# The forgetting attention's causal mask: a sum on DVE and GpSimd at the diagonal blocks in place of a TensorE product

## Chip, cores and metric

One core of a Trainium2 chip runs the whole program. The metric is the device time of one execution in microseconds (us). The engines are named as the profile names them: PE (TensorE products), PEld (its weight loads), DVE (VectorE), ACT (ScalarE), POOL (GpSimd), SP (the queue that issues the loads).

## What is computed

Two transformer blocks follow each other. The first has two layers; in each, half of the mixed width is a gated linear attention ("gla") and the other half a forgetting attention ("fox") with 8 heads of 64 over 528 positions (16 meta positions and 512 of the sequence). Only the fox part is touched:

```python
def forgetting_attention(q, k, v, log_f):
    c = jnp.cumsum(log_f.astype(jnp.float32), axis=1)
    ...
    def block(inp):
        q_b, c_b, start = inp
        logits = (jnp.einsum('bqhd,bkhd->bhqk', q_b, kf)
                  + c_b[..., None] - c_k[:, :, None, :])
        q_pos = start + jnp.arange(Q_BLOCK)
        logits = jnp.where(key_pos[None, :] <= q_pos[:, None], logits, -jnp.inf)
        return jnp.einsum('bhqk,bkhd->bqhd', jax.nn.softmax(logits, axis=-1), vf)
```

A query's own gate `c_b` is the same for all its keys and falls out of the softmax, so the kernel adds the keys' gates `-c_k` and the causal mask alone.

## The kernel before

The program is a list of projection jobs. A job multiplies eight 128-row slices of a weight by the activations: `steps` (L321) issues, for each slice, three products over two halves of 264 positions, since every fp32 factor is split into a high and a low part. Loading and splitting the weights of later jobs (L272 on ACT, L273 on DVE) runs ahead of them. Between the slices `pump` takes functions from a queue and so strews the attention's small work over the projections. The final order on each engine is then made by a scheduler that works with its own model of durations; each engine runs its list in that order, and waits are put in where data or buffers demand them. Tiles named `g` come from a common pool of 64 SBUF buffers, score tiles (`foxS`) from a pool of two PSUM buffers.

The forgetting attention works on pairs of heads `p` (four per layer). Per pair, `fox_gates` multiplies a selector by the gates' sum (L550) and has ACT copy the result to SBUF (L552): `st["cb"][b]`, 128 equal rows with minus the gate of each key, for head `b` of the pair. `fox_pair` then queues ten units per pair: `fox_unit(b, j)` for two heads and five query blocks, j = 0 (the 16 meta queries) and j = 1 to 4 (128 queries each, N = 144, 272, 400 and 528 keys). That is 80 units in both layers, 64 of them with j of 1 or more. A unit has three stages. Its stages are queued so that the scores of one unit stand ahead of the transposes of the one before:

- `scores`: two products (L512, L513) add up q times the keys' high and low parts in PSUM; for j = 4 this is done in two score tiles (272 and 256 keys). A third product, of a bf16 identity and `maskb` (L572), adds -1e30 above the diagonal to the last 128 columns. DVE then adds the gates, writes the negative logits to `P` and reduces their minimum in one instruction (L573, shown as CUSTOM_DVE_ANT_0, with a short instruction behind it that reads the accumulator out). With two score tiles the second starts from the first's minimum. ACT takes the exponential and its sum (L577).
- `trans`: PE transposes P (L602 for the sequence keys, L610 for the first 128 keys; L582 for j = 0), ACT and DVE split the result into high and low parts (L607, L611, L179).
- `values`: for j = 2 and 4, PE multiplies by the values (L622), ACT and DVE put the halves together (L624, L626).

On POOL stand small jobs of the same stage: zeros (L495, L596, L538), the reciprocal roots of the norms (L187) and a subtraction with a repeated operand (L435).

The code of the functions concerned:

Of the kernel before, what the change touches and what calls it, by code (L numbers as in the profile page):

```python
# [12 lines left out]
ALU = mybir.AluOpType  # L13
AX = mybir.AxisListType

META = 16
# [20 lines left out]
class Net:  # L37
# [503 lines left out]

    def fox_gates(self, st, p):
        nc = self.nc
        st["cb"] = []
        for b in range(2):
            cb = self.G()
            for a, n in ((0, HALF), (HALF, L - HALF)):
                ps = self.PS("foxC_")
                self.pin(
                    nc.tensor.matmul(ps[:, :n], lhsT=self.sel[:, 2 * p + b, :], rhs=self.c3[:, a:a + n],  # L550
                                     start=True, stop=True))
                nc.scalar.activation(cb[:, a:a + n], ps[:, :n], AF.Copy)  # L552
            st["cb"].append(cb)

    def fox_unit(self, st, b, j, group):

        nc = self.nc
        r = 64 * b
        q0, qs = BLK[j] if j else (0, 128)
        N = q0 + qs  # L560
        parts = [(0, N)] if N <= 512 else [(0, HALF), (HALF, N - HALF)]
        u = {}

        def scores():
            P, mx = self.G(), self.S()
            col = st["sums"][:qs, 2 * j + b:2 * j + b + 1]
            for x, (a, n) in enumerate(parts):
                ps = self.PS("foxS_")
                last = a + n == N
                self.stacked_scores(ps, st["q"][b], st["kh"][b], st["kl"][b], q0, a, max(n, 256), not last)  # L570
                if last:
                    nc.tensor.matmul(ps[:, n - qs:n], lhsT=self.identb, rhs=self.maskb[:, :qs], start=False, stop=True)  # L572
                nc.vector.tensor_tensor_reduce(P[:qs, a:a + n], ps[:qs, :n], st["cb"][b][:qs, a:a + n], -1.0,  # L573
                                               3.0e38 if x == 0 else mx[:qs, 0:1], op0=ALU.add, op1=ALU.min,
                                               accum_out=mx[:qs, x:x + 1])
            m = mx[:qs, len(parts) - 1:len(parts)]
            nc.scalar.activation(P[:qs, :N], P[:qs, :N], AF.Exp, scale=-1.0, bias=m, accum_out=col)  # L577
            u["P"] = P

        def trans_meta():  # L580
            pm = self.PT("foxT_")
            nc.tensor.transpose(pm[:, :128], u["P"][:, :128], self.ident)  # L582
            PM = self.M()
            nc.vector.tensor_copy(PM, pm[:, :128])
            rc = self.S()
            nc.vector.reciprocal(rc[:META, 0:1], st["sums"][:META, b:b + 1])
            o = self.PT("foxV_")
            nc.tensor.matmul(o[:, :64], lhsT=PM, rhs=st["vm"][:, r:r + 64], start=True, stop=True)
            nc.vector.tensor_scalar(st["O"][:META, 0, r:r + 64], o[:META, :64], rc[:META, 0:1], None, op0=ALU.mult)

        def trans():
            odd = j % 2
            if odd:
                for z in "hl":
                    group[z] = [self.G(F32R)[:, :512].rearrange("p (k c) -> p k c", k=2) for _ in range((j + 1) // 2)]
                    nc.gpsimd.tensor_tensor(group[z][j // 2][:, 1, 0:128], self.ident, self.ident, op=ALU.subtract)  # L596
                group["m"] = self.G(F32R)[:, :512].rearrange("p (z c) -> p z c", z=2)
            C = slice(0, 128) if odd else slice(128, 256)
            pt = self.PT("foxT_")
            for k in range(1, j + 1):  # L600
                b0, _ = BLK[k]
                nc.tensor.transpose(pt[:, 128 * (k - 1):128 * k], u["P"][:, b0:b0 + 128], self.ident)  # L602
            pv = pt[:, :128 * j].rearrange("p (k c) -> p k c", k=j)
            for x in range(0, j, 2):
                n = min(2, j - x)
                h = group["h"][x // 2][:, :n, C]
                nc.scalar.activation(h, pv[:, x:x + n], AF.Copy)  # L607
                self.lo_sub(group["l"][x // 2][:, :n, C], pv[:, x:x + n], h)
            pm = self.PT("foxT_")
            nc.tensor.transpose(pm[:, :128], u["P"][:, :128], self.ident)  # L610
            nc.scalar.activation(group["m"][:, 0, C], pm[:, :128], AF.Copy)  # L611
            self.lo_sub(group["m"][:, 1, C], pm[:, :128], group["m"][:, 0, C])

        def values():

            vs, vms = st["vs"][b], st["vms"][b]
            o = self.PT("foxV_")
            ops = [(vms, group["m"][:, 0, :]), (vms, group["m"][:, 1, :])]
            for k in range(j):
                ops += [(vs[:, 128 * k:128 * k + 128], group[z][k // 2][:, k % 2, :]) for z in ("h", "l")]  # L620
            for x, (lt, rv) in enumerate(ops):
                nc.tensor.matmul(o[:, :256], lhsT=lt, rhs=rv, start=x == 0, stop=x == len(ops) - 1)  # L622
            tmp = self.G()
            nc.scalar.activation(tmp[:64, :256], o[64:, :256], AF.Copy)  # L624
            c0 = 128 * (j - 2)
            nc.vector.tensor_tensor(st["oT"][r:r + 64, c0:c0 + 256], o[:64, :256], tmp[:64, :256], op=ALU.add)  # L626

        if j == 0:
            return [scores, trans_meta]
        return [scores, trans] if j % 2 else [scores, trans, values]  # L630

    def fox_pair(self, st, i, p, mix, last):
# [1041 lines left out]
```

## Time and profile before

| | us |
|---|---|
| median of 3 runs | 2336.28 (2336.06 to 2337.36) |
| the profiled execution, its own time | 2338.46 |
| its span, first to last instruction | 2336.7 |
| PE busy in the span | 2311.3 |
| DVE busy | 1369.9 |
| ACT busy | 953.3 |
| POOL busy | 254.4 |

How it is read: busy time of PE runs from the first column of a product to its modelled end, and products overlap, so the time that a product takes out of PE's stream is read from the distance between the starts of its neighbours and not from its own duration. The fox units lie in two stretches, from 68 to 230 us (first layer) and from 735 to 897 us (second layer). A row of the view by windows gives the stretch, its length, the busy time and number of instructions of PE, PEld, DVE, ACT and POOL, and then the granted clock as a share of full speed, the DMA share and GB/s.

### The profile page before, as it was taken

How to read it: one execution, taken by the hardware profiler on the slowest of the kernel's cores; microseconds unless marked ns; L12 is line 12 of the kernel's file. 1: busy time of each engine (PE TensorE's matmuls, PEld its weight loads, DVE VectorE, ACT ScalarE, POOL GpSimd, SP SyncE). 2: the span in 40 equal slices, each digit the busy share in tenths (PEclk: the TensorE clock that was granted, in tenths of full speed). 3: DMA queues.
4: the chain of work that ended last, by engine and by line, in shares of the span. 5: the costliest groups of instructions: out<-in, count | busy, mean ns of one | idle time of the engine just before them, and what ended most of it. 6: DMA issues, size and time to landing. Idle time of an engine off the chain costs nothing.

```text
span 2336.7 us, 37580 instructions
## 1 busy us (share of the span) xinstructions
PE 2311.3 (99%) x15703; PEld 2126.2 (91%) x15703; DVE 1369.9 (59%) x2445; ACT 953.3 (41%) x1641; POOL 254.4 (11%) x261
## 2 busy tenths in 40 slices
PE   8999999999999999999999999999999999999998
PEld 7999999999999999999999889988999888888888
DVE  6767656465657677465565666796454454433335
ACT  6665534233347556343233534222333533322225
POOL 2111210000022112200000221100000002101012
PEclk9999999999999999999999999999999999999999
DMA  4211222222232211222223222232221222323324
GB/s 116 73 55 55 73 90 86 95 87 87 87 88 71 57 55 52 94 91 91 91 82 106 85 78 82 92 98 91 73 73 55 73 93 92 104 90 90 99 86 131
DMA packets 217072, 196.77 MB, mean 84 GB/s; under 512 B 8987, under 2 KB 214791, under 8 KB 216903
## 3 DMA queue, kind: packets, MB, share of 16 engines
q1 hardware_dynamic: 216903, 194.37, 26.7%
q8 instruction: 124, 2.03, 0.4%
q14 instruction: 45, 0.37, 0.1%
HBM read 192.26 MB, written 2.10 MB: 83 GB/s over the span
## 4 chain that ended last, share of the span: by engine, by line
PE 67%; ACT 1%; DVE 1%; issue 1%; DMA 0%; POOL 0%; POOLq 0%; ACTq 0%; SPq 0%; DVEq 0%
PE mm L321 60%; PE valuesT L1160 1%; PE scoresS L1143 1%; PE foxV L622 1%; PE attend_pT L482 1%; PE foxT L602 0%; PE foxS L512 0%; PE foxS L513 0%; DMA raw<-in_w_down_dram 0%; PE idx L512 0%; ACT wh L272 0%; PE spreadS L221 0%; PE idx L513 0%; DVE g L432 0%; PE token_sumsT L210 0%
## 5 line engine op out<-in xcount | busy, mean ns | idle before, releaser
L321 PE MATMUL mm<-g,wh 128*128 128x264 f32 (+3 forms) x9168 | 1879.0, 315 | 3.1 <-ACT wh L272 1.4
L321 PEld LDWEIGHTS mm<-g,wh 128*128 128x128 f32 x9168 | 1388.2, 189 | 103.7 <-ACT wh L272 1.7
L321 PE MATMUL mm<-g,wl 128*128 128x264 f32 (+3 forms) x4552 | 1160.0, 313 | 0.0
L321 PEld LDWEIGHTS mm<-g,wl 128*128 128x128 f32 x4552 | 750.5, 189 | 50.4
L272 ACT ACTIVATE wh<-raw 128x1024 fp32r<-128x1024 f32 (+1 forms) x369 | 384.8, 1043 | 934.2 <-PE mm L321 797.3
L273 DVE TENSOR_TENSOR wl<-raw,wh 128x1024 fp32r<-128x1024 f32 (+1 forms) x369 | 444.9, 1206 | 74.6 <-ACT wh L272 64.2
L377 DVE TENSOR_TENSOR g<-mm,g 128x528 f32<-128x528 f32 (+2 forms) x228 | 158.7, 696 | 319.7 <-PE mm L321 315.1
L204 POOL TENSOR_TENSOR g<-g,g 128x528 f32<-128x528 f32 (+3 forms) x49 | 71.6, 1472 | 900.5 <-ACT g L203 900.5
L179 DVE TENSOR_TENSOR g<-g,g 128x512 fp32r<-128x512 f32 (+3 forms) x131 | 91.7, 700 | 37.9 <-ACT g L1012 29.2
L1037 DVE TENSOR_TENSOR g<-mm,g 128x528 f32<-128x528 f32 (+1 forms) x48 | 33.6, 700 | 119.3 <-PE mm L321 119.2
L994 ACT ACTIVATE g<-g,cv 128x528 f32<-128x528 f32 (+1 forms) x88 | 72.2, 820 | 17.9 <-DVE g L377 17.7
L1423 POOL TENSOR_TENSOR g<-g,g 128x512 f32<-128x512 f32 x22 | 38.8, 1766 | 283.1 <-ACT g L1422 283.1
L997 DVE SCALAR_TENSOR_TENSOR g<-g,cv,g 128x526 f32<-128x526 f32 (+1 forms) x88 | 66.8, 760 | 3.1
L996 DVE SCALAR_TENSOR_TENSOR g<-g,cv,g 128x527 f32<-128x527 f32 (+1 forms) x88 | 66.4, 754 | 1.8 <-ACT g L994 1.8
L179 DVE TENSOR_TENSOR g<-foxT,g 128x128 fp32r<-128x128 f32 (+1 forms) x160 | 50.5, 340 | 20.3 <-ACT g L607 18.1
L1008 ACT ACTIVATE g<-g 128x528 f32<-128x528 f32 (+1 forms) x44 | 28.1, 639 | 83.8 <-DVE g L997 83.8
L187 POOL TENSOR_TENSOR sm<-sm,mhalf 128x10 f32<-128x10 f32 (+3 forms) x29 | 37.2, 1291 | 116.8 <-DVE sm L186 115.7
L1010 DVE TENSOR_TENSOR g<-g,g 128x528 f32<-128x528 f32 (+1 forms) x44 | 30.8, 701 | 32.3 <-ACT g L1008 32.3
L577 ACT ACTIVATE g<-g,sm 128x144 f32<-128x144 f32 (+2 forms) x80 | 43.1, 538 | 15.5 <-DVE sm L573 14.7
L607 ACT ACTIVATE g<-foxT 128x256 fp32r<-128x256 f32 (+1 forms) x96 | 33.2, 346 | 27.7 <-PE foxT L602 22.7
L1012 ACT ACTIVATE g<-g 128x528 fp32r<-128x528 f32 (+1 forms) x44 | 28.1, 639 | 33.1 <-DVE g L1010 33.1
L1454 DVE TENSOR_TENSOR g<-mm,g 128x512 f32<-128x512 f32 x16 | 11.1, 692 | 49.9 <-PE mm L321 49.9
(281 smaller groups left out, 1697.5 us busy)
## 6 DMA issues: line engine op xcount, KB each, us to landing
raw<-in_w_up_dram SPq DMA_DIRECT2D x50, 1024.0 KB
raw<-in_w_in_dram SPq DMA_DIRECT2D x44, 1024.0 KB
raw<-in_w_down_dram SPq DMA_DIRECT2D x28, 896.0 KB
raw<-in_w_in_dram SPq DMA_DIRECT2D x28, 512.0 KB
raw<-in_w_out_dram SPq DMA_DIRECT2D x12, 1024.0 KB
raw<-in_w_down_dram SPq DMA_DIRECT2D x12, 1024.0 KB
raw<-in_w_gate_dram SPq DMA_DIRECT2D x10, 1024.0 KB
raw<-in_w_up_dram SPq DMA_DIRECT2D x10, 512.0 KB
```

The costliest lines, as they stand in the source:

```text
L179: (eng or self.nc.vector).tensor_tensor(out, x, hi.bitcast(F32), op=ALU.subtract)
L187: self.nc.gpsimd.tensor_tensor(out, v[:rows, :n], self.mhalf[:rows, :n], op=ALU.pow)
L204: nc.gpsimd.tensor_tensor(acc[:, t0:t1], tmp[:, t0:t1], acc[:, t0:t1], op=ALU.add)
L272: keep(nc.scalar.activation(hi[:, :K], src, AF.Copy))
L273: keep(nc.vector.tensor_tensor(lo[:, :K], src, hi[:, :K].bitcast(F32), op=ALU.subtract))
L321: nc.tensor.matmul(ps[:, b, :n], lhsT=w[:, k, :], rhs=x[:, t:t + n], start=(ki == 0 and pi == 0), stop=(ki == len(order) - 1 and pi == len ...
L377: self.nc.vector.tensor_tensor(self.v(out, toks), self.psv(ps, toks), self.v(rs, toks), op=ALU.mult)
L577: nc.scalar.activation(P[:qs, :N], P[:qs, :N], AF.Exp, scale=-1.0, bias=m, accum_out=col)
L994: nc.scalar.activation(A[:, lo:], U[:, lo:], AF.Identity, bias=self.vec("cb", 44 * i + t), scale=cw(2))
L996: nc.vector.scalar_tensor_tensor(A[:, s1:], U[:, s1 - 1:L - 1], cw(1), A[:, s1:], op0=ALU.mult, op1=ALU.add)
L997: nc.vector.scalar_tensor_tensor(A[:, s0:], U[:, s0 - 2:L - 2], cw(0), A[:, s0:], op0=ALU.mult, op1=ALU.add)
L1423: nc.gpsimd.tensor_tensor(z[:, META:], z[:, META:], self.rs[:, META:], op=ALU.mult)
```

## The change

`fox_gates` makes a second tile per head, `cm`: the gates `cb` plus the causal mask `fmask` (-3e38 above the diagonal), repeated over the four 128-key blocks, by one POOL instruction of 128 x 512. In `scores` the product with `maskb` stays for j = 0 alone. For j of 1 or more the last 128 columns are cut off: DVE adds `cb` to the columns ahead of them and `cm` to these, each by an instruction of its own with its own accumulator read, the later one starting from the minimum of the earlier. Nothing else is edited.

```diff
     def fox_gates(self, st, p):
-        st["cb"] = []
+        st["cb"], st["cm"] = [], []
...
             st["cb"].append(cb)
+            cm = self.G()
+            nc.gpsimd.tensor_tensor(cm[:, META:].rearrange("p (j c) -> p j c", j=4),
+                                    cb[:, META:].rearrange("p (j c) -> p j c", j=4),
+                                    self.fmask.unsqueeze(1).to_broadcast([128, 4, 128]), op=ALU.add)
+            st["cm"].append(cm)
...
-            for x, (a, n) in enumerate(parts):
+            x = 0
+            for a, n in parts:
                 ps = self.PS("foxS_")
-                last = a + n == N
-                self.stacked_scores(ps, st["q"][b], st["kh"][b], st["kl"][b], q0, a, max(n, 256), not last)
-                if last:
+                mask = j == 0
+                self.stacked_scores(ps, st["q"][b], st["kh"][b], st["kl"][b], q0, a, max(n, 256), not mask)
+                if mask:
                     nc.tensor.matmul(ps[:, n - qs:n], lhsT=self.identb, rhs=self.maskb[:, :qs], start=False, stop=True)
-                nc.vector.tensor_tensor_reduce(P[:qs, a:a + n], ps[:qs, :n], st["cb"][b][:qs, a:a + n], -1.0,
-                                               3.0e38 if x == 0 else mx[:qs, 0:1], op0=ALU.add, op1=ALU.min,
-                                               accum_out=mx[:qs, x:x + 1])
-            m = mx[:qs, len(parts) - 1:len(parts)]
+
+                cuts = [(a, n, "cb")]
+                if j and a + n == N:
+                    cuts = [(a, n - qs, "cb"), (N - qs, qs, "cm")] if n > qs else [(a, n, "cm")]
+                for c, w, key in cuts:
+                    nc.vector.tensor_tensor_reduce(P[:qs, c:c + w], ps[:qs, c - a:c - a + w], st[key][b][:qs, c:c + w],
+                                                   -1.0, 3.0e38 if x == 0 else mx[:qs, x - 1:x], op0=ALU.add,
+                                                   op1=ALU.min, accum_out=mx[:qs, x:x + 1])
+                    x += 1
+            m = mx[:qs, x - 1:x]
```

The lists of PE, DVE, ACT and POOL change between the first fox scores of a layer and the start of its output projection; SP's does not change, and PE's is the same everywhere else. In the changed file the lines behind the edit are higher by 5 to 12: L573 becomes L584, L602 L614, L610 L622, L622 L634, L596 L608; L578 is the mask product that is left.

PE's list before, first layer, first pair of heads, from the scores of the unit b = 0, j = 3 (`foxS_1024`) on; `foxT_992` and `foxT_996` are the transposes of the unit ahead of it:

```order
L512 MATMUL foxS_1024<-g_646,g_713 128x400
L513 MATMUL foxS_1024<-g_647,g_713 128x400
L572 LDWEIGHTS identb
L572 MATMUL foxS_1024<-maskb,identb 128x128
L321 MATMUL mm_957<-g_288,wh_721 128x264 x2
L321 MATMUL mm_957<-g_289,wh_721 128x264
L602 MATMUL foxT_992<-ident,g_928 128x128
```

And after, the same place (`foxS_1028` is that unit's tile, `foxT_996` and `foxT_1000` are the transposes ahead):

```order
L512 MATMUL foxS_1028<-g_646,g_713 128x400
L513 MATMUL foxS_1028<-g_647,g_713 128x400
L321 MATMUL mm_961<-g_288,wh_721 128x264 x2
L321 MATMUL mm_961<-g_289,wh_721 128x264 x2
L321 MATMUL mm_961<-g_288,wl_722 128x264 x2
L321 MATMUL mm_961<-g_313,wh_721 128x264 x2
L614 MATMUL foxT_996<-ident,g_932 128x128
```

The weight load and the product of the mask are gone, and the earlier unit's transposes stand behind eight projection products where they stood behind three.

DVE's list before at the same place, from the last split of the earlier unit's transposes:

```order
L626 TENSOR_TENSOR g_807<-foxV_1006,g_1013 64x256
L573 ISA g_1022,sm_1023<-foxS_1024,g_815 128x400
L573 ISA sm_1023 128x1
L179 TENSOR_TENSOR g_989<-foxT_1036,g_987 128x2x128
L179 TENSOR_TENSOR g_991<-foxT_1041,g_991 128x128
L573 ISA g_1051,sm_1052<-foxS_1053,g_815 128x272
```

And after (`g_815` is `cb`, `g_822` is `cm` of head b = 0):

```order
L638 TENSOR_TENSOR g_807<-foxV_1010,g_1017 64x256
L584 ISA g_1026,sm_1027<-foxS_1028,g_815 128x272
L584 ISA sm_1027 128x1
L179 TENSOR_TENSOR g_993<-foxT_1040,g_991 128x2x128
L584 ISA g_1026,sm_1027<-foxS_1028,g_822,sm_1027 128x128
L584 ISA sm_1027 128x1
L179 TENSOR_TENSOR g_995<-foxT_1045,g_995 128x128
```

One sum over 400 columns has become one over 272 and one over 128, and a split of another unit's transposes stands between them.

POOL's list before, first pair of the first layer (L427 finishes the gates' sum, L596 are zeros for the values' stage):

```order
L427 TENSOR_TENSOR c_110<-g_526,g_596 8x528
L495 MEMSET g_653 64x528
L596 TENSOR_TENSOR g_909<-ident 128x128
L596 TENSOR_TENSOR g_911<-ident 128x128
L495 MEMSET g_939 64x528
```

And after:

```order
L427 TENSOR_TENSOR c_110<-g_526,g_596 8x528
L495 MEMSET g_653 64x528
L555 TENSOR_TENSOR g_822<-g_815,fmask 128x512
L555 TENSOR_TENSOR g_831<-g_824,fmask 128x512
L608 TENSOR_TENSOR g_913<-ident 128x128
L608 TENSOR_TENSOR g_915<-ident 128x128
L495 MEMSET g_943 64x528
```

The two sums of mask and gates stand ahead of the pair's zeros; in the rest of the list the other 14 are put in in the same way and nothing else moves.

## Rows read from the trace of the kernel before

**Rows 1.** The page, part 1: busy time of each engine over the span.

```profile
PE 2311.3 (99%) x15703; PEld 2126.2 (91%) x15703; DVE 1369.9 (59%) x2445; ACT 953.3 (41%) x1641; POOL 254.4 (11%) x261
```

**Rows 2.** The page, part 4: the chain that ended last, shares by engine.

```profile
PE 67%; ACT 1%; DVE 1%; issue 1%; DMA 0%; POOL 0%; POOLq 0%; ACTq 0%; SPq 0%; DVEq 0%
```

**Rows 3.** Fox stretches by window: length, then each engine's busy us (and instructions).

```profile
68.00:230.00 162.00, 160.99 (x1292) 152.34 (x1291) 117.74 (x340) 94.80 (x257) 24.95 (x44) 1.00 0.18 51
735.00:897.00 162.00, 161.12 (x1293) 152.60 (x1294) 118.02 (x341) 94.65 (x257) 24.76 (x43) 1.00 0.19 55
```

**Rows 4.** The mask product as a group by line: busy us, mean ns.

```profile
L572 PE MATMUL foxS<-maskb,identb 128*128 128x128 bf16 x80 | 18.4, 229 | 0.0
```

**Rows 5.** PE in order of time (start, length), with and without mask, both 272 columns.

```profile
157.87 0.29 PE L512 MATMUL foxS<-g,g 128*128 128x272 f32 x1
...
158.12 0.23 PE L572 MATMUL foxS<-maskb,identb 128*128 128x128 bf16 x1
158.16 0.73 PE L321 MATMUL mm<-g,wh 128*128 128x264 f32 x4
158.73 0.40 PE L321 MATMUL mm<-g,wl 128*128 128x264 f32 x2
158.97 0.52 PE L321 MATMUL mm<-g,wh 128*128 128x264 f32 x3
...
213.05 0.29 PE L512 MATMUL foxS<-g,g 128*128 128x272 f32 x1
...
213.30 0.65 PE L321 MATMUL mm<-g,wh 128*128 128x264 f32 x4
213.79 0.40 PE L321 MATMUL mm<-g,wl 128*128 128x264 f32 x2
214.03 0.65 PE L321 MATMUL mm<-g,wh 128*128 128x264 f32 x4
```

**Rows 6.** PE in order of time, a mask product with transposes behind it.

```profile
73.05 0.23 PE L572 MATMUL foxS<-maskb,identb 128*128 128x128 bf16 x1
73.12 0.28 PE L602 MATMUL foxT<-ident,g 128*128 128x128 f32 x1
73.24 0.27 PE L610 MATMUL foxT<-ident,g 128*128 128x128 f32 x1
73.27 0.74 PE L321 MATMUL mm<-g,wh 128*128 128x264 f32 x4
```

**Rows 7.** DVE groups of L573 by shape: busy us, mean ns, idle before.

```profile
L573 DVE CUSTOM_DVE_ANT_0 g<-foxS,g 128x272 f32<-128x272 f32 x32 | 13.8, 433 | 4.0 <-PE foxS L572 3.9
L573 DVE CUSTOM_DVE_ANT_0 g<-foxS,g 128x400 f32<-128x400 f32 x16 | 9.0, 561 | 0.0
L573 DVE DVE_READ_ACCUMULATOR2_ANT sm<- 128x1 f32 x96 | 7.9, 82 | 0.0
L573 DVE CUSTOM_DVE_ANT_0 g<-foxS,g,sm 128x256 f32<-128x256 f32 x16 | 7.7, 479 | 0.6
L573 DVE CUSTOM_DVE_ANT_0 g<-foxS,g 128x144 f32<-128x144 f32 x16 | 4.8, 302 | 1.2 <-PE foxS L572 0.7
```

**Rows 8.** All engines in order of time: an exponential and the transposes behind it.

```profile
82.60 0.62 ACT L577 ACTIVATE g<-g,sm 128x400 f32<-128x400 f32 x1
...
83.44 0.49 PE L602 MATMUL foxT<-ident,g 128*128 128x128 f32 x3
```

**Rows 9.** PE's waits, the fox stage's: total us, times, longest.

```profile
PE foxV L522 <- DVE g L377: 2.2, 3, 1.9
...
PE foxT L602 <- ACT g L611: 0.2, 1, 0.2
```

**Rows 10.** ACT and DVE in time, first pair; POOL's sum with a repeated operand as group.

```profile
68.36 0.36 ACT L552 ACTIVATE g<-foxC 128x256 f32<-128x256 f32 x1
...
70.72 0.31 DVE L573 CUSTOM_DVE_ANT_0 g<-foxS,g 128x144 f32<-128x144 f32 x1
...
L435 POOL TENSOR_TENSOR g<-g 128x512 f32<-128x512 f32 x4 | 5.8, 1438 | 5.8 <-DVE g L432 4.0 <-DVE g L437 1.7
```

## Prediction

> **What bounds the kernel now.** I read the page's first part first: PE is busy 99% of the span, DVE 59%, ACT 41%, POOL 11% [rows 1]. The chain that ended last lies on PE for 67% of the span, and no other engine has more than 1% of it [rows 2]. So time is won by taking work out of PE's stream, or lost by making PE wait. The change touches two stretches of 162 us. The view by windows shows both alike, which is as it should be, as both layers run the same code: PE busy 161 of 162 us at full clock, DVE 118, ACT 95, POOL 25 [rows 3]. What I looked for next was what one mask product takes out of that stream, and how far DVE's answer lies ahead of the transposes that need it. The waits of PE in the fox stage are short: 0.2 us in all for the transposes, 2.2 us for those of the values, and these wait for an eviction and not for the softmax [rows 9].
>
> **What is removed.** 64 of the 80 mask products (j of 1 or more), each with its weight load. The record of one says 229 ns [rows 4], but records overlap, so the price is the distance between neighbours. Two units with 272 columns give it. Without a mask (the first half of a j = 4 unit) the stretch from L512 over L513 and six projection products to the next one is 214.03 - 213.05 = 0.98 us. With the mask it is 158.97 - 157.87 = 1.10 us, six products again [rows 5]. The difference is 0.12 us. It falls in two pieces: the product behind the mask starts 0.04 us after it (158.16 - 158.12), but its group of four takes 158.73 - 158.16 = 0.57 us where the unmasked group takes 213.79 - 213.30 = 0.49 us. What the 0.08 us are made of the rows don't say, but they come with the mask and only there. Going through the 64 in order of time I find a projection product behind 52 and a transpose behind 12. For those the distance is 73.12 - 73.05 = 0.07 us, and the next transpose starts after 0.12 us [rows 6], some 0.01 more than elsewhere; I take 0.08 us. Sum: 52 x 0.12 + 12 x 0.08 = 6.2 + 1.0 = **7.2 us** off PE. The bounds: 64 x 0.04 = 2.6 us if only the first piece goes, and 64 x 0.229 = 14.7 us if the whole record counted; the latter I exclude, as rows 5 show the overlap.
>
> The Trainium skill has a figure for this (TensorE: Matmul & The Clock Gate, Back-to-back issue gap): about 81 ns for a product of 128 columns in a stream of loads and products, about 56 ns for one by itself. By these the sum would be an estimated 5.2 or 3.6 us; the trace's 0.12 us is more, and I go by the trace.
>
> **What is added on DVE.** Each of the 64 units gets one more sum and one more accumulator read. From 144 to 400 columns a sum goes from 302 to 561 ns, so 1.01 ns for a column and 156 ns for the instruction; the form that starts from an earlier minimum takes 479 ns at 256 columns, 64 ns more than that line; the read takes 82 ns [rows 7]. A cut of 128 columns with such a start is then 156 + 129 + 64 = 349 ns. For j = 2: 302 + 82 + 349 in place of 433, 0.30 us more. The other j give the same within 0.01 us. All together 64 x 0.30 = 19.2 us, 9.6 in each stretch. DVE goes from 118 to some 128 us of 162 [rows 3]: still far from full, and this is the cover. What it costs if the cover is gone is what PE's transposes wait for. The tightest place of the trace: an exponential ends at 82.60 + 0.62 = 83.22 us, and its transposes start at 83.44 [rows 8], 0.22 us later. Of the 64 units 10 have less than 0.55 us there, the others 0.65 to 27 us. If the 0.30 us passed on whole, two of them would be short by 0.08 us. In the new list of PE, however, the transposes at that kind of place have moved back (behind eight projection products instead of three), while in DVE's list a split now stands between the two sums of a unit, which adds to its delay. I take **0.5 us** for the two; if all ten paid whole it would be 3.0 us.
>
> **What is added on POOL.** 16 sums of 128 x 512 with a repeated operand, as L435, which takes 1.44 us [rows 10]: 23 us, on an engine busy 25 of 162 us. DVE waits for them in its own order, and behind it its evictions for PE. In the first pair ACT finishes the last piece of both heads' gates at 68.36 + 0.36 = 68.72 us; both sums one after the other from there end at 71.6, even without counting that the first head's are ready earlier. The first unit's masked piece is wanted at 70.72 plus the short first piece [rows 10] and needs the first sum only, done by 70.2 at the latest; the second head's first masked unit is queued two units further on. Price nought; the pair's zeros behind them on POOL are not wanted before the values. If each of the 8 pairs paid one sum, 8 x 1.44 = 11.5 us.
>
> **What is moved.** PE's list is rearranged in the two stretches, by tens of products at most, and meets the old one before the output projection. PE is idle for 1.0 and 0.9 us in them [rows 3], so a better order can give back 1.9 us at most; a worse one could double them, so also 1.9 us the other way. I take nought and keep both ends. No load is issued elsewhere, since SP's list stays.
>
> **The sum.** 7.2 - 0.5 = 6.7 us saved. It stands against the profiled execution (2338.46 us, span 2336.7), 2.2 us above the median; nothing in the two stretches hangs on that difference, so I take the saving off the median: 2336.28 - 6.7 = **2329.6 us**, 0.29% less.
>
> **The rivals.**
> - *The second piece stays.* The 0.08 us behind a mask belong to any change of the kind of product, and with the mask gone the time is lost elsewhere in the stream, so that only the first piece, 2.6 us, is won: 2333.7 us. For it: the two kinds still alternate at every transpose. Against it: the unmasked row of rows 5 has no such piece.
> - *The longer softmax holds PE now and then.* Each unit that is late costs up to 0.30 us; with 20 of 64 late, 7.2 - 6.0 = 1.2 us are left: 2335.1 us. For it: DVE's list strews other splits between a unit's sums. Against it: the slack of rows 8, small for 10 units only.
> - *DVE becomes the bound of the stage (slower).* If the two-buffer score tiles, now released later by the added sum, and the late exponentials make PE wait for the whole added 0.30 us in every unit, the loss is 19.2 us against 7.2: 2336.28 + 12.0 = 2348.3 us. It decides from 24 late units of 64 (7.2 / 0.30). For it: all scores pass through two buffers. Against it: DVE idles 44 of 162 us. The Trainium skill (VectorE: DVE Perf Modes, Rules for kernel authors) advises to lower the number of DVE instructions, as each flushes its pipe; the trace's 156 ns per instruction agrees.
> - *The change doesn't do what it says.* PE's new list has 16 mask products, those of j = 0, and no others; I give it nothing.
>
> **How the numbers follow.** A measurement of this kernel tells about 0.2%, 4.7 us, from no change. Forecast 0.63; second piece stays 0.14; late now and then 0.14; DVE the bound 0.06; and 0.03 for more than the forecast, a better order giving its 1.9 us and the mask 0.13 us (2326 us). The forecast's own range is 6.7 less the 1.9 us of the rearrangement and a little more, to 6.7 + 1.9: 2327.7 to 2331.5, all beyond 4.7 us. So faster 0.63 + 0.03 = 0.66; same 0.14 + 0.14 = 0.28; slower 0.06. To hold 8 in 10 the range needs most of the two middle rivals: 2327.5 to 2335.0 us.
>
> **What would show it.** Right: 16 records of the mask product; L512 to the product seven places on 0.98 us in j = 2 units as in unmasked ones; the fox stretches shorter by 3.3 us each and the rest unchanged; some 128 us of DVE in each; POOL's new sums near 1.4 us and done before the first sum over `cm`; PE's waits for the transposes still under 1 us in all. Wrong: waits of PE on L589's exponential or on the release of score tiles; sums over `cm` that start on POOL's release; stretches that are shorter by 1.3 us only.

## The result and the profile after

| | before | after |
|---|---|---|
| median, us | 2336.52 (6 runs, 2336.06 to 2339.97) | 2349.07 (6 runs, 2347.64 to 2351.09) |
| ratio | 1 | 1.0051 [1.0041, 1.0061] |

The changed kernel is slower by 0.51%, 12.6 us between the medians, where 6.7 us less was forecast. The page (part 1, against [rows 1]) and the windows of the fox stretches (against [rows 3]):

```profile
PE 2310.9 (98%) x15639; PEld 2127.0 (91%) x15639; DVE 1378.2 (59%) x2573; ACT 952.0 (41%) x1641; POOL 273.6 (12%) x277
```

```profile
68.00:230.00 162.00, 160.06 (x1262) 151.40 (x1262) 122.20 (x401) 93.48 (x254) 38.13 (x59) 1.00 0.20 57
735.00:897.00 162.00, 160.04 (x1259) 151.15 (x1258) 122.08 (x394) 93.06 (x252) 39.41 (x59) 1.00 0.19 55
```

In each of these windows PE idles 1 us more than before, which explains no 12 us. The loss lies just behind them. PE's waits in the fox stage (us in total, times, longest); L522 waited as long before [rows 9], the others are new:

```profile
PE foxN L695 <- DVE o L682: 4.8, 2, 2.4
PE foxV L634 <- DVE g L179: 4.5, 2, 2.3
...
PE foxV L522 <- DVE g L377: 2.2, 3, 1.7
...
PE mm L321 <- DVE g L379: 1.1, 2, 0.5
...
PE to_tokensT L708 <- DVE gvm L176: 0.7, 2, 0.4
```

Each of the new ones comes once in each layer, the two long ones (L695, L634) at the end of the last pair of heads, the two short ones further ahead. The first of the long ones in time is that of the last values. DVE, ACT and PE there (start, length, and in brackets the idle time before and who ended it):

```profile
232.44 0.42 DVE L179 TENSOR_TENSOR g<-foxT,g 128x256 fp32r<-128x256 f32 x1
233.60 1.22 DVE L273 TENSOR_TENSOR wl<-raw,wh 128x1024 fp32r<-128x1024 f32 x1 [0.74 <-ACT wh L272]
234.74 0.61 DVE L179 TENSOR_TENSOR g<-foxT,g 128x256 fp32r<-128x256 f32 x2
...
232.51 1.06 ACT L272 ACTIVATE wh<-raw 128x1024 fp32r<-128x1024 f32 x1
233.48 0.36 ACT L619 ACTIVATE g<-foxT 128x256 fp32r<-128x256 f32 x1
...
235.31 0.77 PE L634 MATMUL foxV<-g,fvms 128*128 128x256 f32 x2 [2.27 <-DVE g L179]
```

A later job's weight split (L272 on ACT, then L273 on DVE) stands between the splits of the last unit, and PE waits 2.27 us for the last of these. Before, that weight split stood nine microseconds later, at 242.84 us. The second wait is 15 us further on. DVE and POOL, then PE:

```profile
243.65 0.68 DVE L768 TENSOR_REDUCE sm<-g 128x4 f32<-128x512 f32 x1
246.13 0.69 DVE L776 TENSOR_TENSOR g<-g,sm 128x512 f32<-128x512 f32 x1 [1.81 <-POOL sm L187]
...
248.02 0.69 DVE L776 TENSOR_TENSOR g<-g,sm 128x512 f32<-128x512 f32 x1 [0.80 <-POOL sm L187]
248.63 0.70 DVE L377 TENSOR_TENSOR g<-mm,g 128x528 f32<-128x528 f32 x1
...
249.32 0.82 DVE L682 TENSOR_TENSOR o<-o,sm 128x640 f32<-128x640 f32 x1
...
243.18 2.92 POOL L187 TENSOR_TENSOR sm<-sm,mhalf 128x10 f32<-128x10 f32 x2 [0.17 <-DVE sm L186]
246.98 1.01 POOL L187 TENSOR_TENSOR sm<-sm,mhalf 128x4 f32<-128x4 f32 x1 [0.88 <-DVE sm L186]
...
250.28 0.74 PE L695 MATMUL foxN<-ident,o 128*128 128x128 f32 x5 [2.42 <-DVE o L682]
```

The scaling of the fox result (`fox_scale`, L682) stands behind two gla scalings (L776), and each of these waits for a power on POOL (1.81 and 0.80 us). PE's transposes (L695) wait 2.42 us. In the kernel before the order is the other way round, the fox scaling first:

```profile
240.89 0.83 DVE L670 TENSOR_TENSOR o<-o,sm 128x640 f32<-128x640 f32 x1
...
244.05 0.69 DVE L764 TENSOR_TENSOR g<-g,sm 128x512 f32<-128x512 f32 x1
```

A third part of the loss is the clock behind the first wait (windows; granted clock is the third number from the end):

```profile
225.00:230.00 5.00, 5.00 (x44) 4.77 (x43) 3.66 (x16) 3.46 (x11) 0.00 (x0) 1.00 0.44 153
230.00:235.00 5.00, 3.04 (x25) 2.62 (x23) 2.38 (x5) 2.26 (x5) 0.00 (x0) 0.98 0.00 0
235.00:240.00 5.00, 4.69 (x25) 4.37 (x26) 2.08 (x5) 2.14 (x4) 0.00 (x0) 0.68 0.01 2
...
245.00:250.00 5.00, 2.86 (x24) 2.64 (x22) 3.07 (x7) 1.72 (x5) 2.62 (x4) 1.00 0.00 0
```

From 235.3 us on PE works without a break and yet does 25 products up to 240 us, where it did 44 from 225 to 230: by the granted clock 3.4 us, from 234.8 us on, are at 1.2 GHz in place of 2.4. The second layer shows the same (0.66 from 907 to 912 us).

What the change was meant to do it does. The mask product is left for j = 0 alone; an unmasked j = 2 unit takes 113.40 - 112.42 = 0.98 us; the sums on DVE and POOL cost what [rows 7, 10] let one expect. PE in order of time:

```profile
112.42 0.29 PE L512 MATMUL foxS<-g,g 128*128 128x272 f32 x1
...
113.40 0.40 PE L321 MATMUL mm<-g,wh 128*128 128x264 f32 x2
```

And the groups of the mask product, DVE's sums and POOL's sums by line and shape (count, busy us, mean ns, idle before):

```profile
L578 PE MATMUL foxS<-maskb,identb 128*128 128x128 bf16 x16 | 3.7, 230 | 0.0
...
L584 DVE CUSTOM_DVE_ANT_0 g<-foxS,g,sm 128x128 f32<-128x128 f32 x80 | 27.2, 345 | 3.0 <-PE foxS L513 0.9
L584 DVE DVE_READ_ACCUMULATOR2_ANT sm<- 128x1 f32 x160 | 13.0, 82 | 0.0
L555 POOL TENSOR_TENSOR g<-g,fmask 128x512 f32<-128x512 f32 x16 | 20.3, 1288 | 153.0 <-DVE fvms L179 55.7 <-ACT g L552 50.8 <-PE foxC L550 36.3
```

### The profile page after: what moved, and what is told of

Same layout as the page of the kernel before. It is cut to its first block, busy times and chain, and to the rows that moved or that the text cites. A ratio compares the mean times of both kernels' runs of the same rounds, so it can differ in the third digit from the quotient of the medians.

```text
span 2349.0 us, 37654 instructions
## 1 busy us (share of the span) xinstructions
PE 2310.9 (98%) x15639; PEld 2127.0 (91%) x15639; DVE 1378.2 (59%) x2573; ACT 952.0 (41%) x1641; POOL 273.6 (12%) x277
## 4 chain that ended last, share of the span: by engine, by line
PE 66%; DVE 1%; ACT 1%; issue 1%; DMA 0%; POOL 0%; POOLq 0%; ACTq 0%; SPq 0%; DVEq 0%
PE mm L321 60%; PE valuesT L1172 1%; PE scoresS L1155 1%; PE foxV L634 1%; PE attend_pT L482 1%; PE foxT L614 0%; PE foxS L512 0%; DVE wl L273 0%; DMA raw<-in_w_down_dram 0%; ACT wh L272 0%; PE foxS L513 0%; PE idx L512 0%; PE to_tokensT L465 0%; PE idx L513 0%; PE spreadS L221 0%
## 5 line engine op out<-in xcount | busy, mean ns | idle before, releaser
L321 PE MATMUL mm<-g,wh 128*128 128x264 f32 (+3 forms) x9168 | 1878.1, 315 | 4.1 <-ACT wh L272 1.4
L321 PEld LDWEIGHTS mm<-g,wh 128*128 128x128 f32 x9168 | 1392.0, 189 | 103.8 <-ACT wh L272 1.7
L321 PE MATMUL mm<-g,wl 128*128 128x264 f32 (+3 forms) x4552 | 1158.3, 313 | 0.0
L321 PEld LDWEIGHTS mm<-g,wl 128*128 128x128 f32 x4552 | 751.0, 189 | 49.6
L272 ACT ACTIVATE wh<-raw 128x1024 fp32r<-128x1024 f32 (+1 forms) x369 | 384.7, 1043 | 920.4 <-PE mm L321 778.4
L273 DVE TENSOR_TENSOR wl<-raw,wh 128x1024 fp32r<-128x1024 f32 (+1 forms) x369 | 445.1, 1206 | 77.8 <-ACT wh L272 67.7
```

The lines of the kernel that those rows point to most:

```text
L272: keep(nc.scalar.activation(hi[:, :K], src, AF.Copy))
L273: keep(nc.vector.tensor_tensor(lo[:, :K], src, hi[:, :K].bitcast(F32), op=ALU.subtract))
L321: nc.tensor.matmul(ps[:, b, :n], lhsT=w[:, k, :], rhs=x[:, t:t + n], start=(ki == 0 and pi == 0), stop=(ki == len(order) - 1 and pi == len ...
```

## The experiments

**The measure.** All kernels run the same 13,720 projection products (L321) in the same order. A layer's fox part with the end of its last pair lies between the starts of the 211th and the 1401st (first layer), and of the 4901st and the 6301st (second). These two times, from each kernel's trace, the time at half clock within them, and the ratio to runs of before on the same chip:

| kernel | first, us | second, us | half clock, us | median of the runs | ratio to before |
|---|---|---|---|---|---|
| before | 227.19 | 249.56 | 3.4 + 0 | 2336.52 | 1 |
| before, again | 225.67 | 249.47 | 0 + 0 | 2337.76 | 1.0002 [0.9992, 1.0012] |
| changed | 231.99 | 256.28 | 3.4 + 3.4 | 2349.07 | 1.0051 [1.0041, 1.0061] |
| changed, again | 232.13 | 255.99 | 3.4 + 3.4 | 2348.04 | 1.0050 [1.0035, 1.0065] |
| product out | 223.69 | 247.62 | 0 + 0 | 2329.00 | 0.9966 [0.9954, 0.9978] |
| product out, again | 224.06 | 247.66 | 0 + 0 | 2329.69 | 0.9968 [0.9956, 0.9981] |
| sum cut | 226.70 | 250.81 | 0 + 0 | 2338.54 | 1.0006 [0.9997, 1.0015] |
| no POOL sums | 231.35 | 254.08 | 3.4 + 0 | 2345.26 | 1.0042 [1.0029, 1.0054] |
| both places | 226.68 | 251.20 | 0 + 0 | 2339.20 | 1.0010 [1.0001, 1.0018] |
| scale ahead | 228.67 | 253.73 | 3.4 + 3.4 | 2342.53 | 1.0025 [1.0016, 1.0034] |
| split behind | 230.92 | 255.23 | 3.4 + 3.4 | 2345.00 | 1.0035 [1.0021, 1.0048] |
| tail restored | 226.77 | 251.20 | 0 + 0 | 2335.82 | 0.9999 [0.9990, 1.0008] |
| last pair by products | 225.23 | 249.62 | 0 + 0 | 2336.65 | 0.9999 [0.9990, 1.0008] |
| whole masked gates | 225.62 | 250.25 | 0 + 0 | 2336.00 | 0.9998 [0.9989, 1.0007] |

The two profiles of the kernel before give the price of one piece at half clock: 227.19 - 225.67 = 1.5 us. Sums below are against the second one, 225.67 + 249.47 = 475.1 us.

**The product alone.** Before, with `last` in `scores` true for j = 0 only:

```diff
-                last = a + n == N
+                last = a + n == N and j == 0
```

> The kernel before without its 64 mask products of j = 1 to 4, and nothing in their place (so the causal mask inside the diagonal blocks is left out of the result). DVE, ACT and POOL have their old work, and their lists differ from the old ones by 46, 26 and no rows; the end of the last pair stands in the old order. It prices the product alone. By the prediction's term it is 7.2 us faster than before (2329.3 us, ratio 0.997). By the account of the two traces it is little: between the same two projection products the changed kernel's first stretch is 4.8 us longer with 5.45 us more idle time of PE, the second 6.9 us longer with 5.72 us more idle time and one more piece at half clock (3.4 us, so 1.7 us lost), which leaves 0.65 and 0.5 us for the products: 1.2 us faster (2335.3 us, 0.9995). If the removal alone brought the loss, it is slower by up to 12 us.

> The kernel before without its 64 mask products once more (the causal mask inside the diagonal blocks is left out of the result). Between the same projection products its two stretches were 1.8 and 1.9 us shorter than those of the kernel before, after taking 1.7 us off for the latter's piece at half clock: 3.7 us, while the medians differ by 8.0 us. If the product is worth 8 us, it is at 2328 to 2330 us again, with few pieces at half clock. If only the 3.7 us belong to it and the rest was chance, it is at 2331 to 2334 us here.

Measured twice: 8.0 and 7.7 us faster. The stretches are 3.8 and 3.4 us shorter, so 3.6 us on average. The account made from the changed kernel's trace (1.2 us in all) falls. The price of one product is what was predicted, 0.98 us for a unit that took 1.10, but part of the 7.2 us is given back in small waits of PE for the units' splits, which the trace of before has not or not so long [rows 9]. First profile of this kernel:

```profile
PE foxV L522 <- DVE g L377: 2.4, 3, 1.8
PE foxT L602 <- DVE g L179: 1.4, 5, 0.3
PE foxV L622 <- DVE g L179: 0.5, 2, 0.3
```

PE idles 6.9 us (4.1 + 2.8) in these two stretches, against 4.8 us (2.9 + 1.9) in the second profile of before: 2.1 us are given back so. A listed wait is counted from the modelled end of the product ahead; in the changed kernel the last product ahead of the wait of 2.27 us starts 2.56 us before the next, where products in a stream start 0.12 us apart, so 2.44 us are lost, 0.17 us more than listed. By this the seven new waits are an estimated 1.2 us longer than listed, and 3.6 + 2.1 + 1.2 = 6.9 us, near the 7.2.

Another 4 us of the difference of the medians these stretches don't show. 1.4 us of it is a piece at half clock near 693 us, which both profiles of before have and both of this kernel have not, behind a wait of 0.8 us that all four have. The granted clock of all runs points the same way: its mean is 0.9973 in the 37 runs of before on the two chips that this kernel ran on, and 0.9985 in this kernel's 12, so before is at half clock for some 2 x 0.0012 x 2330 = 5.6 us more. At 1.5 us for a piece of 3.4 us that is an estimated 2.5 us at most (the 1.4 among them), and so a part of the 8 us is clock and not the products' own time. Why the clock falls less often is open, and so is what is left of the 4 us.

**DVE's part alone.** Before, products kept, the sum cut:

```diff
-            for x, (a, n) in enumerate(parts):
+            x = 0
+            for a, n in parts:
...
+                cuts = [(a, n)]
+                if j and last and n > qs:
+                    cuts = [(a, n - qs), (N - qs, qs)]
+                for c, w in cuts:
```

> The kernel before with its mask products kept, and the last 128 columns of each unit's sum on DVE cut off into an instruction of their own with its accumulator read, as the change has them, over the unmasked gates. It is DVE's part alone, and the end of the last pair stands in the old order. If the added work of DVE (19 us) is what slows the changed kernel, it is 10 us or more slower than before (2347 us, ratio 1.004 or more). If the order at the end of the last pair does it, DVE's part alone costs 0 to 2 us (2336 to 2338 us, 1.000 to 1.001).

1.5 us slower by the medians, with an interval of the ratio that holds 1, and 2.4 us in the stretches (1.0 + 1.3). The added work of DVE alone is not what costs 12 us.

**POOL's part.** The changed kernel with `st["cm"].append(cb)` in place of the sum over `fmask`.

> The changed kernel without POOL's 16 sums: the cut-off sum reads the unmasked gates (so the causal mask inside the diagonal blocks is left out of the result). PE, DVE and ACT have the changed kernel's work, and the weight split and the fox scale stand at the end of the last pair where the changed kernel has them. If POOL's sums hold DVE or PE, it is back at 2330 to 2337 us (ratio to before 0.998 to 1.000). If the order does it, it stays within 2 us of the changed kernel: 2347 to 2351 us (1.0045 to 1.0062).

Still 8 us slower than before, with the same two waits. In the stretches, pieces at half clock taken off, it is 483.9 us against 485.2: POOL's 16 sums cost 1.3 us with the order that comes with them, not nothing, but not the loss. Most of it is the wait for L379 (1.1 us), which this kernel doesn't have. The median is 1.7 us under the expected range; 1.5 us of that is the piece at half clock that the second stretch doesn't have in this profile.

**The order put back at both places.** No work is changed; edges tell the scheduler what to place behind what. `fs` is the instruction of `fox_scale`, and `late` holds the last unit's splits on ACT and DVE:

```diff
     def split(self, jb, pin=False):
...
+            with ExitStack() as es:
+                for x in late[0] + late[1]:
+                    es.enter_context(self.tc.issue_after(x.ins))
+                nc.scalar.activation(hi[:, :K], src, AF.Copy)
+                nc.vector.tensor_tensor(lo[:, :K], src, hi[:, :K].bitcast(F32), op=ALU.subtract)
...
         def scale():
+            with self.tc.issue_after(self.fs.ins):
```

The first edge is on the one weight split that had come forward, the second on the gla scales. The next two kernels have the second edge alone and the first alone. In the traces of all three every engine's order is the changed kernel's up to 232 us and from 271 us on (904 and 942 us in the second layer), and POOL's is the same throughout.

> The changed kernel with two orders put back, in each layer: the weight split that went ahead of the last unit's splits stands behind them (on ACT and DVE), and the fox scale stands ahead of the gla scales that wait for POOL. Work and data are the changed kernel's. If the order at these two places does it, PE's waits there (2.27 + 2.42 us in the first layer, about as much in the second) and the piece at half clock behind the first go: 9.4 us of waits and some 3.4 us of clock, so 12 us less than the changed kernel, 2336 to 2338 us (ratio to before 1.000 to 1.001) if the product is worth about 1 us, and 2330 to 2333 us if it is worth 7. If DVE's or POOL's added work does it, it stays at 2345 us or more.

> The changed kernel with the fox scale put back ahead of the gla scales on DVE, and nothing else; the weight split stays ahead of the last unit's splits. If each of the two places costs what PE waits there, PE's wait for the fox scale (2.42 us and 2.36) goes and that for the last values (2.27 twice) stays: 5 us less than the changed kernel, 2344 us (ratio to before 1.003). If the first wait alone brings the rest with it, nothing is won: 2348 to 2350 us.

> The changed kernel with the weight split put behind the last unit's splits on ACT and DVE, and nothing else; the fox scale stays behind the gla scales. PE's wait for the last values shrinks from 2.27 us to about 0.45 (as in the run with both places), the half-clock piece behind it (3.4 us, 1.7 us lost) goes, and a wait of 1.1 us for the eviction behind the split stays, twice: 4 to 6 us less than the changed kernel, 2343 to 2345 us (ratio to before 1.0025 to 1.0035). With the run before, the two savings should add up to the 9.9 us of both places. If they don't add up, the second wait takes over what the first gives.

With both, 9.9 us of the 12.6 are back by the medians (2339.2 us, 1.2 above the expected range), with the changed kernel's DVE and POOL work untouched. So the order at the end of the last pair is the cause of the larger part. Of the single ones, the fox scale put ahead brings 6.5 us, 1.5 more than expected, the split put behind 4.1. The stretches tell more: there they bring 5.9 and 2.1 us, each with two pieces at half clock still in them, and both edges 10.4 us, with none. 3.0 of the 10.4 us are the clock, and 7.4 are left against 5.9 + 2.1: the waits' savings add up, but the clock comes back only when both waits go. One expectation on the second fell: the piece at half clock doesn't go, it moves behind the other wait. PE with the split behind:

```profile
233.57 0.50 PE L647 MATMUL foxV<-g,fvms 128*128 128x256 f32 x2 [0.45 <-DVE g L180]
236.35 0.64 PE L331 MATMUL mm<-g,wh 128*128 128x264 f32 x3 [1.11 <-DVE g L387]
247.53 0.74 PE L708 MATMUL foxN<-ident,o 128*128 128x128 f32 x5 [2.26 <-DVE o L695]
```

The wait for the values (L647 here) shrinks from 2.27 to 0.45 us, that for the eviction behind the weight split (1.11 us) takes part of its place, and the half clock starts at 249.0 us, 1.5 us behind the end of the wait for the fox scale.

**The whole end restored.** As both places, but the weight split behind the fox scale, where it stood before.

> The changed kernel with the whole end of the last pair on DVE in the order of the kernel before: the fox scale ahead of the gla scales, and the weight split behind the fox scale (on ACT behind the square), so that an eviction that PE waits for (1.1 us a layer with both places mended) doesn't stand behind the split either. If the order at the end is what is left, PE loses 1.3 to 2.0 us less in each layer than with both places mended (2339.2 us): 2335 to 2336.5 us (ratio to before 0.999 to 1.000). If what is left lies in the middle of the stage or in DVE's added work, it stays at 2338 to 2340 us.

The median is as expected, 2335.8 us, and the wait of 1.11 us is gone. But the stretches are not shorter than with both places mended (226.77 and 251.20), and the intervals of the two ratios overlap, so the 3.4 us between the medians can't be put down to that wait. What is left against product and cut together, 478.0 - (475.1 - 3.6 + 2.4) = 4.1 us, holds POOL's 1.3 us, with the wait for L389 (L379 in the changed kernel) in it, and two more waits that the kernel before has not, for the last values (L647) and at `to_tokens` (L721):

```profile
PE mm L331 <- DVE g L389: 1.1, 2, 0.5
PE foxV L647 <- DVE g L180: 0.9, 2, 0.4
PE to_tokensT L721 <- DVE gvm L177: 0.7, 2, 0.4
```

**The last pair by products.** The changed kernel, with the change left out for the last of the four pairs, so that the end falls into its old order by itself. POOL still makes all 16 sums.

> The changed kernel with the last of the four pairs of heads masked by products as before: 48 of the 64 products are gone and 48 of the sums are cut, and the order at the end of the stage is the old one. If the loss belongs to the order there, three quarters of the product's 8.0 us less the cut's 1.5 us are won, 4.9 us, and up to 2.6 us are lost at two waits in the middle of the stage: 2332 to 2335 us (ratio to before 0.998 to 0.999). If DVE's or POOL's work does it, three quarters of the loss stay: 2346 us (1.004).

The loss is gone, as it must be if the order is its cause, and the two long waits too, but the gain doesn't come: 2336.65 us, 1.7 above the expected range. The expectation was reckoned with the 8.0 us between medians. With what the stretches show, three quarters of 3.6 us are won and of 2.4 us lost, and the wait at `to_tokens` (0.7 us in all) is there: 475.1 - 2.7 + 1.8 + 0.7 = 474.9 us, and 474.9 us were measured.

**Fewer cuts.** POOL makes two masked copies of a head's gates, so that only j = 1 needs a cut: 16 new sums on DVE in place of 64, 80 instructions on POOL in place of 16. DVE's end is again in the old order.

`zm` holds 128 zero columns and the mask; `ce` gets blocks 2 and 4 masked, `co` block 3, and block 1 at its end:

```diff
-            cm = self.G()
...
+            ce, co = self.G(), self.G()
+            nc.gpsimd.tensor_tensor(co[:, 400:], cb[:, META:META + 128], self.fmask, op=ALU.add)
+            nc.gpsimd.tensor_copy(ce[:, :META], cb[:, :META])
...
+                                    self.zm.unsqueeze(1).to_broadcast([128, 2, 256]), op=ALU.add)
+            nc.gpsimd.tensor_copy(co[:, :144], cb[:, :144])
+            nc.gpsimd.tensor_tensor(co[:, 144:400], cb[:, 144:400], self.zm, op=ALU.add)
```

> All 64 products out, the mask kept, but the sums on DVE cut for j = 1 alone (16 units in place of 64): POOL makes, from the gates of a head, one tile with blocks 2 and 4 masked and one with block 3 masked, so that the sums of j = 2, 3 and 4 read one tile each, as before; POOL has 80 new instructions in place of 16, DVE 34 more than before. The end of the last pair comes out in the old order. If order is the cause of the changed kernel's loss and the added sums cost little, it keeps nearly the gain of the run without products (8.0 us), less a quarter of the cut's 1.5 us and up to 2 us for POOL: 2329.5 to 2332 us (ratio to before 0.997 to 0.998), faster than both kernels. If POOL's added work holds DVE, it is at 2336 us or more.

> The changed kernel once more, on the same chip as the run before, so that the two can be set side by side, and for a second profile of its waits and of the granted clock behind them. The two waits at the end of each layer's last pair (2.27 and 2.4 us) should be there again to within 0.1 us, as they follow from the order; the pieces at half clock may lie elsewhere. 2347 to 2351 us (ratio to before 1.004 to 1.006).

No gain: 2336.0 us, the same as before, where 2329.5 to 2332 us were expected. In the first pair POOL is now busy beside DVE's weight split, and both take longer. DVE and POOL of this kernel in order of time:

```profile
73.97 1.87 DVE L276 TENSOR_TENSOR wl<-raw,wh 128x1024 fp32r<-128x1024 f32 x1
75.76 1.64 DVE L182 TENSOR_TENSOR g<-g,g 64x528 fp32r<-64x528 f32 x2
...
73.64 2.45 POOL L618 TENSOR_TENSOR g<-ident 128x128 fp32r<-128x128 f32 x4
```

And DVE of the kernel without products, where POOL rests there:

```profile
73.62 1.23 DVE L273 TENSOR_TENSOR wl<-raw,wh 128x1024 fp32r<-128x1024 f32 x1
74.76 0.69 DVE L179 TENSOR_TENSOR g<-g,g 64x528 fp32r<-64x528 f32 x1
```

PE then waits for a split (0.95 us at 78.36 us, and 0.99 us in the second layer). In the two stretches PE idles 9.3 us, 2.4 more than without products, and they are 4.6 us longer; what makes the rest is not shown. The Trainium skill says why these two engines may hold each other (GPSIMD Engine Reference, Specifications): POOL's interface to SBUF is shared with DVE, and instructions of DVE with two SBUF inputs contend. Both of DVE's here have two, so the rows agree.

The repeat of the changed kernel has its two waits again at the same places (2.27 and 2.42 us), with the half clock at the first in both layers.

**Before, again.**

> The kernel before once more, for a second profile. The first one has pieces at half clock at 64.0, 695.5 and 1354.3 us, the run without products only at 1346.7 us, and nothing ahead of 64 us differs between the two. If the pieces belong to the kernel (its waits end at 63.8 and 693.8 us), they are there again at the same places. If they fall by chance, other ones are there, or fewer, and the time is 2335 to 2338 us all the same.

The piece at 64 us is not there again, those near 693 and 1352 us are. So a piece behind a given wait comes with some profiles and not with others, and stretches are compared without them.

## Why the prediction was wrong

- **What bounds the kernel**: right. PE is the bound, and time was lost by making it wait.
- **What is removed, 7.2 us**: the 0.12 us of a unit are confirmed, and alone the edit is 8.0 and 7.7 us faster. That this is so near 7.2 is in part luck: in the stretches only 3.6 us are won, as PE then waits more often for splits, which the sum left out, and up to 2.5 us of the medians' difference are clock.
- **What is added on DVE, 0.5 us**: 1.5 us by the medians, 2.4 in the stretches, within the bound of 3.0 but undersized. The sums' sizes were right (345 ns against 349); L584's records add up to 18.7 us more than L573's did, against 19.2. The windows show 122 us of DVE and not 128, since the prediction added durations to a time that counts overlaps once: the records of the first window add up to 141 us (133 before) and cover 122 (118).
- **What is added on POOL, nought**: 1.29 us each, and done in time, as worked out (nothing waits for L555), but 1.3 us in all by the order that comes with the sums.
- **What is moved, nought, 1.9 us either way**: this step failed. The lower end had a reason, PE's idle time. The upper one, "a worse one could double them", had none; no row bounds what a new order may cost. I read the order at the first pair, where the edit stands, and not at the end of the last, where the stage's last results are due on PE and later jobs' work can come to stand ahead of them. DVE's order there tells it: the fox scale stood ahead of all gla scales before, and behind two of them after. What the new order costs is 4.5 + 4.8 = 9.3 us in the two long waits, 1.8 us in the two short ones, and 3.0 us in two pieces at half clock, for which the sum had no term: 14.1 us where 1.9 was the most allowed for.
- **The sum, as it is now**: -3.6 (product) + 2.4 (cuts) + 9.3 + 1.8 + 3.0 = 12.9 us, against 488.27 - 475.14 = 13.1 us measured in the stretches and 12.0 to 12.6 us between the medians. POOL's 1.3 us is not added, as the wait for L379 that makes most of it is among the 1.8. Product and cuts were priced in other orders than the changed kernel's, so that the sum comes out so closely is partly chance.
- **The rivals**: "DVE becomes the bound" gave 2348.3 us, close to the 2349.1 measured, but by a mechanism that the runs refute: DVE's cuts alone cost 1.5 us, and the same DVE work in another order is 9.9 us faster. A time that fits is no proof of its cause. The list of what would show the prediction wrong had no wait for anything but score tiles and exponentials, and the two waits are neither.

What stays open: why the scheduler, given both edits, turns the order at the end round when either edit alone leaves it; and some of the 4 us that the kernel without products gains beyond the stretches. No version that keeps the mask was faster than before by more than the measurement tells.

## What to carry to other kernels

Where a scheduler places the instructions, an edit is priced with the new order or not at all: compare the lists of each engine to the point where they meet again, above all at the end of a chain whose results a busy engine takes, and look for an instruction that has come to stand behind one that waits for a third engine. A gain of a tenth of a microsecond per unit is worth checking against the length of one such wait. A few ordering edges at the places where the waits are can bring back most of it at no cost in work.

## What was not expected of the hardware

- **Half clock at short waits.** PE's granted clock fell to 1.2 GHz for 3.4 us at waits of 2.3 us in the changed kernel: from 234.8 and 907.2 us on, where the waits end at 235.3 and 907.4, in the repeat from 234.9 and 907.3. With the split behind it fell at 249.0 and 918.0 us, behind the waits for the fox scale, and not behind the waits of 0.45 and 1.11 us ahead of them. The length of the wait alone doesn't decide it: near 693 us both profiles of before have it behind a wait of 0.8 us. By the two profiles of before a piece costs 1.5 us. The windows of the repeat show PE idle for most of 3 us and then at work throughout at half speed:

```profile
232.00:235.00 3.00, 0.73 (x5) 0.50 (x4) 2.24 (x5) 1.50 (x3) 0.00 (x0) 0.99 0.00 0
235.00:238.50 3.50, 3.50 (x17) 3.50 (x18) 0.98 (x2) 1.08 (x3) 0.00 (x0) 0.52 0.00 0
```

- **The same wait, with and without it.** The wait of 1.9 us that ends at 63.8 us is followed by half clock in the first profile of before and not in the second, where it is 1.8 us long and ends at 62.8 (windows of the first, then of the second):

```profile
60.00:65.00 5.00, 3.14 (x23) 2.86 (x22) 4.74 (x6) 2.64 (x4) 2.40 (x3) 0.90 0.70 212
```

```profile
60.00:65.00 5.00, 3.17 (x26) 2.87 (x26) 4.61 (x8) 2.65 (x6) 1.44 (x2) 1.00 0.65 210
```

- **DVE and POOL side by side** lengthened a weight split from 1.23 to 1.87 us, and four of POOL's zeros from 1.47 us in the changed kernel (71.02 us, DVE at other work) to 2.45. Not always: of the 4382 weight splits of 128 x 1024 in the 14 traces, none without a TENSOR_TENSOR of POOL beside it took more than 1.23 us, and 75 of the 592 with one did, up to 1.90 us.
